# Bias tables of block 1 repeated inside DRAM, all four at the start, and their transfers issued from the GpSimd queue

## Chip, cores and metric

The kernel runs on one core of a Trainium2 chip. The metric is the device time of one execution in microseconds (us). The reference has one batch row of 512 tokens and 1024 features; everything is float32, and products are made exact enough by splitting each operand into a high part (fp32r) and a low part, three matmuls for one.

## The reference, cut to what matters

Block 1 is a layer with three attention branches and a convolutional feed-forward; block 2 has two more layers. The change touches only block 1's attention. Its first branch has three groups of four heads (dilation 1, 4, 16), its second eight heads with a sliding window; to the logits of all of them a bias is added that depends only on the distance between query and key, by a table of 32 buckets:

```python
def band_bias(table, dist):
    return jnp.transpose(table[t5_bucket(dist)], (2, 0, 1)).astype(jnp.float32)

logits = jnp.einsum('nkgbqd,nkbsd->nkgbqs', qb, kw, preferred_element_type=jnp.float32) * SCALE
logits = jnp.where(mask, logits + bias[:, :, None], -jnp.inf)
m = jnp.max(logits, axis=-1)
p = jnp.exp(logits - m[..., None])
```

Queries go in blocks of 128 against the block before and their own, so the bias of one head is a 128 x 256 matrix in which every diagonal is constant.

## The kernel before

The kernel is written with tiles and pools; a scheduler sets the order in which each engine's instructions stand, and each engine then runs its list in order. Weights come in 512 KB pieces (`wraw`, three buffers, line 153) through the queue of SyncE (SP), are split by ScalarE (ACT, line 139, high part) and VectorE (DVE, line 140, low part) and used by TensorE (PE) in `gemm` (line 172). For a branch there are blocks of 256 columns: queries, keys, values. Values are made token-major in `v_direct` (line 576).

The bias comes in three steps. `bias_rows` multiplies a one-hot matrix (`oh`, 198 KB, and `tb`) on PE (line 468) and DVE copies the four results (line 470), one for each kind of head, into a small `row` tile: 4, 4, 4 and 8 heads, 384 distances each. `bias_table` (line 477) writes each row 128 times into a DRAM tile `fd`: with 4 heads 768 KB, with 8 heads 1536 KB. Read with a step one element shorter than a row, it gives a head's matrix (`bias_ap`); `band_bias` (line 817) and the two reads in `attn_a` (lines 752 and 757) bring it into one of two `tmp_bias` buffers. Then DVE adds it to the scaled scores (line 513, or 545 for dilation 4 and 16), takes the maximum (516, 547), ACT exponentiates (485, 550), PE transposes (491) and multiplies with the values (532, 554).

Table 0 is made before group 0, tables 1 and 2 before their groups, table 3 before the third branch, which has no bias itself, and it is read in the second branch. All these transfers are issued from SP, the queue that also issues the weights. `normed` (lines 715 to 721) makes the normalised input again from `num` tiles, which come through SP as well.

Of the kernel before, what the change touches and what calls it, by code (L numbers as in the profile page):

```python
# [65 lines left out]
class Weights:  # L66
    """[128, 512] tiles (high, low) of a [K, c] block, 512 / c rows of 128 in each"""
# [17 lines left out]
class QWeights:  # L85
    """tiles of the quarters (column tile n, rows k < 4 or k >= 4)"""
# [8 lines left out]
class Builder:  # L95
# [41 lines left out]
    def wsplit(self, raw, H, L):  # L137
        """the exact high and low parts"""
        self.nc.scalar.copy(out=H, in_=raw)  # L139
        self.nc.vector.tensor_sub(out=L, in0=raw, in1=H.bitcast(F32))  # L140

    def wtiles(self, raw, pool=None, tag="wq", bufs=4, cols=1024, step=512, back=False):
        """the parts of up to 1024 columns, 512 by 512"""
        pool, m = pool or self.wp, raw.shape[-1]
        t = [pool.tile([P, cols], F32R, name=tag + x, tag=tag + x, bufs=bufs) for x in "HL"]
        for q in sorted(range(0, m, step), reverse=back):
            self.wsplit(raw[:, q:q + step], *[x[:, q:min(q + step, m)] for x in t])
        return [[x[:, q:q + 512] for x in t] for q in range(0, m, 512)]
# [27 lines left out]
    def strassen_y(self, ys, R, keep=False):  # L176
        """the sums of the quarters of y (rows k < 4 and k >= 4, first and second half of the tokens)"""
        nc, h = self.nc, R.n // 2
        a0, b0 = R.off, R.off + h
        A, B = slice(a0, b0), slice(b0, b0 + h)  # L180
        T, todo = {i: [] for i in (1, 2, 3, 4)}, []
        for k in range(4):
            if self.inplace:
                w = self.x[:, k::4]
                q = [w[:, 0, A], lambda w=w: w[:, 1, A], w[:, :, B]]
            else:
                q = [self.first_half(k, A), lambda k=k: self.first_half(k + 4, A), self.half_y[k][:, :, :h]]
            todo.append(self.y_sums(T, k, *q, None if keep else [t[:, B] for t in ys[k]]))
        for rest in todo:
            rest()  # L190
        half = lambda k, s: [ys[k][0][:, s], ys[k][1][:, s]]
        return [[half(k, A) for k in range(4)], [half(k + 4, A) for k in range(4)], [half(k + 4, B) for k in range(4)],
                T[4], T[1], T[2], T[3]]

    def gemm_pairs(self, W, ys, R, use, between=()):
        """all column tiles; the first two advance together, as the last of ys may come late"""
        nk, per, between = len(ys), KD // len(W), list(between)
        for g in ((0, 1), *((t,) for t in range(2, KD))):
            ps = [[(self.psum("o" if t == 4 else "g"), o, m) for o, m in R.segs] for t in g]
            for k in range(nk):  # L200
                yH, yL = ys[k]
                for t, p in zip(g, ps):
                    H, L = W[t // per].at(k, t % per)
                    for i, (a, b) in enumerate(((H, yH), (H, yL), (L, yH))):
                        for q, o, m in p:
                            self.nc.tensor.matmul(q[:, :m], lhsT=a, rhs=b[:, o:o + m],  # L206
                                                  start=(k == 0 and i == 0), stop=(k == nk - 1 and i == 2))
            if between:
                between.pop(0)()
            for t, p in zip(g, ps):  # L210
                use(p, t)
# [9 lines left out]
    def y_sums(self, T, k, a, c, w, q4, pool=None):  # L221
        """a and c: the rows k < 4 and k >= 4 of the first half of the tokens; w: both of the second half"""
# [25 lines left out]
    def strassen(self, src, Y, R, out, last, off=0, mid=None):  # L248
        """[2 * 128 features, tokens] of a block of weights with seven products of quarters (Winograd's form);
        the last product lies among the next block's, and last takes what it gives"""  # L250
# [15 lines left out]
        def product(i, ps=None, tag="g"):  # L266
            """with ps, added to what is there"""
# [42 lines left out]
    def end(self):  # L310
        """the last product of the block before"""
        tail, self.tail = self.tail, None
        if tail:
            tail()
# [12 lines left out]
    def sumsq(self, acc, src, R, k):  # L327
        """acc += src^2"""
# [27 lines left out]
    def bcast(self, rc, R):  # L356
        """rc, a column for each chunk of tokens, as rows in all partitions"""
# [21 lines left out]
    def prenorm(self, gname, defer=True, inplace=False):  # L379
        """y = x * g is split and the reciprocal of the norm is applied to the products (defer), or y is normalised"""  # L380
# [11 lines left out]
    def prenorm_r(self, R):  # L392
        """the reciprocal of the norm, in all partitions"""
# [24 lines left out]
    def halves(self, parts, products, post, nextw, nparts=None):  # L418
        """the last products before a norm, half of the tokens by half; the second half is normalised in the next phase"""
# [36 lines left out]
    # ---------------------------------------------------------------- block 1  # L456
    def bias_rows(self, pool):
        """the bias of each distance, a row for each head"""
        nc, A = self.nc, self.A
        oh = pool.tile([33, 4, 384], F32, name="oh")  # L460
        nc.sync.dma_start(out=oh, in_=A["onehot"])
        tb = pool.tile([33, 20], F32, name="tb")
        nc.vector.memset(tb[32:33], 1.0)
        nc.sync.dma_start(out=tb[:32], in_=A["rel_bias"])
# [8 lines left out]
    def bias_table(self, kind):  # L473
        """each row 128 times, to be read along its diagonals"""
        row, n = self.fd[kind]
        self.fd[kind] = self.dp.tile([n, P, 384], F32, name=f"fd{kind}")
        self.nc.sync.dma_start(out=self.fd[kind], in_=row.unsqueeze(1).to_broadcast([n, P, 384]))

    def bias_ap(self, kind, h, rows, k0, nk):
        a = self.fd[kind][:, :, :]  # L480
        return bass.AP(tensor=a.tensor, offset=a.offset + h * P * 384 + 127 + k0, ap=[[383, rows], [1, nk]])
# [15 lines left out]
    def band_head(self, qT, kT, base, kbase, V, bias, ops, obase, negm, l, sink=None):  # L497
        """q^T, k^T [64 rows, 512] in natural order; V(kb) the [128, 64] block; previous and own block."""
# [36 lines left out]
    def block_head(self, qT, kT, base, V, bias, ops, negm, l):  # L535
        """four independent 128-blocks"""
# [28 lines left out]
    def v_direct(self, W, ys, rcol, d):  # L565
        """values token-major: block b holds tokens b*128.. (d=1) or b::4 (d=4)"""
# [15 lines left out]
    def v_transposed(self, vTs, bufs=3):  # L582
        """[128 features, 512] tiles -> token-major blocks"""
# [9 lines left out]
    def block1(self):  # L593
        nc, tc, A = self.nc, self.tc, self.A
        w0 = []
        with self.phase("qp") as qp, ExitStack() as ctx:
# [20 lines left out]
            with self.phase("at") as at:  # L617
                self.qp, self.qkb = at, 10
                with self.phase("ap") as ap:
                    self.ap = ap  # L620
                    self.bias_rows(ap)
                    self.bias_table(0)
# [43 lines left out]
    def gates(self, Y, gates):  # L666
        """the gates' products, kept in DRAM until the branches are merged"""
# [11 lines left out]
    def post_tile(self, ps, acc, t, R, add):  # L679
        """collects a tile of the sublayer's output, in the place of x, and its squares"""  # L680
# [8 lines left out]
    def postnorm(self, acc, gpost, R, Rn, xold, xnew):  # L689
        """x = xold + norm(x); the next pre-norm of the tokens Rn"""  # L690
# [14 lines left out]
    def attn_a(self, W, ys, rb, rc, oH, oL):  # L705
# [17 lines left out]
        for g, d in enumerate((1, 4, 16)):  # L723
            if g:
                self.bias_table(g)
# [15 lines left out]
            for t in range(2):  # L741
                ops = self.psum("o")
                for u in range(2):
# [5 lines left out]
                    else:  # L749
                        b = self.tmp("bias", 2, 512)  # L750
                        if d == 4:
                            nc.sync.dma_start(out=b[:, :P], in_=self.bias_ap(1, h, P, P, P))
                        else:
                            nc.vector.memset(b[:, :P], NEG)
                            for r in range(4):
                                s = slice(32 * r, 32 * r + 32)
                                nc.sync.dma_start(out=b[s, s], in_=self.bias_ap(2, h, 32, P, 32))
# [26 lines left out]
        nc.sync.dma_start(out=sel, in_=A["sel4"])  # L784
# [29 lines left out]
    def band_bias(self, kind, h):  # L814
        b = self.tmp("bias", 2, 512)
        for u in range(2):
            self.nc.sync.dma_start(out=b[:, 256 * u:256 * u + 256], in_=self.bias_ap(kind, h, P, 0, 256))
        return b

    def attn_b(self, W, ys, oH, oL, pool, gate):  # L820
# [4 lines left out]
        nc.sync.dma_start(out=snk[:, 0], in_=A["sinks"].to_broadcast([P, 8]))  # L825
# [30 lines left out]
    def attn_c(self, W, ys, oH, oL):  # L856
        nc, qp, A = self.nc, self.qp, self.A
        self.bias_table(3)
        tri = self.ap.tile([P, P], F32, name="tri")
        nc.sync.dma_start(out=tri, in_=A["tri"])  # L860
        cm = self.ap.tile([P, P], BF16, name="cm")
        cmf = self.tmp("p", 6, 512)
        nc.sync.dma_start(out=cmf[:, :P], in_=A["cmask"])
# [13 lines left out]
    def stick_pair(self, q, k, V, t, ops, tri, cm):  # L877
        """two heads; the blocks j of 128 keys against the queries from j*128 on lie one after the other"""
# [71 lines left out]
    def conv_ffn(self):  # L950
# [5 lines left out]
        def conv(u, j):  # L956
            """u holds two zeros before the first token"""
# [84 lines left out]
    def last_w(self, src, nk=4, spare=("t3",)):  # L1042
        """nk rows of 128 for all columns, in two blocks; what the ring doesn't hold lies where the sums of y were"""
# [19 lines left out]
    def ffn_order(self, chunks, up, down, last):  # L1063
        """the down products of a chunk lie between the up products of the next one"""
# [15 lines left out]
    def flush(self):  # L1080
        """the elementwise rest of a block follows the products of the next one"""
# [4 lines left out]
    def hidden(self, src, dst):  # L1086
        """the parts of two hidden tiles"""
# [7 lines left out]
    # ---------------------------------------------------------------- block 2  # L1095
# [91 lines left out]
    def first_blocks(self, name, ys, R, gs):  # L1187
        """the first blocks in halves of the tokens, so that the second half has time to be normalised"""
# [135 lines left out]
    def feature_major(self, o, base, R):  # L1324
        """transposes [tokens, 128] blocks; yields (psum, first token, tokens) within the range R"""
# [71 lines left out]
    def stack(self, t, R, key):  # L1397
        """the two maps' exact parts for products of K = 128: the queries' high and low parts against the keys' high
        part twice, and the high part against the keys' low part"""
# [13 lines left out]
    def v_heads(self, ps, rb, c0):  # L1413
        """one head's values, token-major; chunks of 128 tokens, the 16-token chunk is slot 4"""
# [18 lines left out]
    def diff_heads(self, heads, lam, R):  # L1433
        """the steps of the blocks of 128 queries: scores(i + 1), values(i - 1), transposes(i)"""
# [106 lines left out]
class Cols:  # L1541
    """[128, 1] column views: t[:, i] or t[:, i, h]"""
# [11 lines left out]
# ------------------------------------------------------------------ host side: layout and shape-only constants  # L1554
def wblocks(w, c=256):
    """[K, N] -> [N/c, 128, (K/128)*c]"""
# [4 lines left out]
def qblocks(w):  # L1561
    """[1024, N] -> [N/256, 128, (column tile, half of the rows, 4, 128)]"""
# [140 lines left out]
```

## Time and profile before

| | us |
|---|---|
| median of 3 runs | 3174.17 (3173.94 to 3175.4) |
| span of the profiled execution | 3173.5 |
| PE busy | 3105.4 (98%) |
| DVE busy | 2250.6 (71%) |
| ACT busy | 1533.8 (48%) |

The span runs from the first to the last instruction of the profiled execution; the median of the runs lies 0.7 us above it, and the profiled execution's own time is taken as 3174.2. PE is the bound on average, so a change can gain only where PE is idle or runs at the lower clock. In the rows below "x" is a count of instructions, "<-" points from what is written to what is read, and a trailing bracket gives the idle time of the engine before the instruction and what ended it.

### The profile page before, as it was taken

Reading aid. Unit: us, or ns where it says so; the run is one execution under the profiler, and the core shown is the slowest. Engines: PE = TensorE matmul, PEld = TensorE weight load, DVE = VectorE, ACT = ScalarE, POOL = GpSimd, SP = SyncE. Lnnn points to the kernel's source line nnn. Section 1 sums busy time; section 2 is a strip of 40 time slices with the busy share of each in tenths; the row PEclk is TensorE's granted clock in tenths of the full one; section 3 lists DMA queues with packets and bytes.
Section 4 is the critical chain, followed back from the end, with each engine's and each line's share of the span. In section 5 each row is a group of like instructions: output and inputs, shape, how many; then the busy total and the mean of one; then the engine's idle time right before and its main releaser. Section 6 shows DMA issues by size and latency. Waiting matters only on the chain.

```text
span 3173.5 us, 54811 instructions
## 1 busy us (share of the span) xinstructions
PE 3105.4 (98%) x22264; PEld 2872.8 (91%) x22264; DVE 2250.6 (71%) x4225; ACT 1533.8 (48%) x2968; POOL 0.7 (0%) x6
## 2 busy tenths in 40 slices
PE   5899999999999999999999999999999999999998
PEld 4676798988899999999889999999999988899998
DVE  4235777887888797775766777768777576677775
ACT  3345555665455554444553444445444455344443
POOL 0000000000000000000000000000000000000000
PEclk8899999999999999999999999999999999999999
DMA  4421236423233332333212223333233321223332
GB/s 120 95 78 62 81 123 204 145 87 111 89 102 110 102 107 94 107 98 104 66 52 64 87 88 106 94 100 94 94 107 95 107 67 59 67 84 106 96 108 77
DMA packets 102148, 304.36 MB, mean 96 GB/s; under 512 B 12387, under 2 KB 27367, under 8 KB 101896
## 3 DMA queue, kind: packets, MB, share of 16 engines
q1 hardware_dynamic: 98296, 294.38, 30.0%
q10 hardware_dynamic: 3600, 6.49, 0.7%
q8 instruction: 174, 2.85, 0.4%
q14 instruction: 78, 0.64, 0.1%
HBM read 286.41 MB, written 14.42 MB: 95 GB/s over the span
## 4 chain that ended last, share of the span: by engine, by line
PE 93%; DMA 4%; DVE 2%; ACT 1%; issue 0%; SPq 0%; DVEq 0%; ACTq 0%
PE ps_g L172 35%; PE ps_g L278 18%; PE ps_g L276 9%; PE ps_s L172 8%; PE ps_g L206 7%; PE ps_o L276 4%; PE ps_o L206 1%; DMA fd<-row 1%; PE ps_g L576 1%; DMA wraw<-in_w_in 1%; PE ps_s L1467 1%; DMA tmp_bias<-fd 1%; PE ps_s L510 1%; PE ps_s L1524 1%; PE ps_o L1503 1%; PE ps_o L532 1%
## 5 line engine op out<-in xcount | busy, mean ns | idle before, releaser
L140 DVE TENSOR_TENSOR wqL<-wraw,wqH 128x512 fp32r<-128x512 f32 (+1 forms) x676 | 604.8, 910 | 275.3 <-ACT wqH L139 267.4
L139 ACT CAST wqH<-wraw 128x512 fp32r<-128x512 f32 (+1 forms) x676 | 526.7, 796 | 495.6 <-PE ps_g L172 258.6
L172 PE MATMUL ps_g<-yH,wqH 128*128 128x264 f32 (+2 forms) x1520 | 430.4, 322 | 2.3 <-ACT wqH L139 2.2
L172 PE MATMUL ps_g<-yL,wqH 128*128 128x264 f32 (+2 forms) x1520 | 430.8, 321 | 0.4 <-DVE yL L414 0.4
L172 PE MATMUL ps_g<-yH,wqL 128*128 128x264 f32 (+2 forms) x1520 | 430.3, 322 | 0.8 <-DVE wqL L140 0.7
L278 PE MATMUL ps_g<-t,wqH 128*128 128x256 f32 (+1 forms) x1760 | 326.5, 283 | 0.0
L172 PEld LDWEIGHTS ps_g<-yL,wqH 128*128 128x128 f32 x1520 | 264.7, 189 | 24.9 <-issue 5.2
L172 PEld LDWEIGHTS ps_g<-yH,wqL 128*128 128x128 f32 x1520 | 263.1, 189 | 23.4 <-issue 4.1
L172 PEld LDWEIGHTS ps_g<-yH,wqH 128*128 128x128 f32 x1520 | 263.4, 189 | 22.6 <-ACT wqH L139 3.1
L278 PEld LDWEIGHTS ps_g<-t,wqH 128*128 128x128 f32 x1760 | 272.4, 188 | 1.8
L278 PE MATMUL ps_g<-t,wqL 128*128 128x256 f32 (+1 forms) x880 | 248.7, 283 | 0.0
L139 ACT CAST wqH<-ws 128x1024 fp32r<-128x1024 f32 x100 | 105.2, 1052 | 126.8 <-PE ps_o L276 34.3
L278 PEld LDWEIGHTS ps_g<-t,wqL 128*128 128x128 f32 x880 | 166.1, 189 | 0.0
L276 PE MATMUL ps_g<-t,wqH 128*128 128x264 f32 (+1 forms) x800 | 148.5, 283 | 0.0
L172 PE MATMUL ps_s<-hL,wqH 128*128 128x264 f32 (+1 forms) x544 | 141.4, 317 | 0.0
L172 PE MATMUL ps_g<-hL,wqH 128*128 128x264 f32 (+1 forms) x544 | 141.3, 317 | 0.0
L172 PE MATMUL ps_g<-hH,wqL 128*128 128x264 f32 (+1 forms) x544 | 141.2, 317 | 0.0
L172 PE MATMUL ps_s<-hH,wqL 128*128 128x264 f32 (+1 forms) x544 | 141.2, 317 | 0.0
L172 PE MATMUL ps_g<-hH,wqH 128*128 128x264 f32 (+1 forms) x544 | 141.1, 317 | 0.0
L172 PE MATMUL ps_s<-hH,wqH 128*128 128x264 f32 (+1 forms) x544 | 141.0, 317 | 0.0
L258 DVE TENSOR_TENSOR ws<-wraw 128x512 f32<-128x512 f32 x100 | 69.3, 693 | 86.9 <-DMA wraw<-in_ffn_w_gate 34.7
L140 DVE TENSOR_TENSOR wqL<-ws,wqH 128x1024 fp32r<-128x1024 f32 x100 | 122.4, 1224 | 6.6 <-ACT wqH L139 3.1
(434 smaller groups left out, 8207.9 us busy)
## 6 DMA issues: line engine op xcount, KB each, us to landing
wraw<-in_ffn_w_gate SPq DMA_DIRECT2D x88, 512.0 KB, 3.7
wraw<-in_ffn_w_up SPq DMA_DIRECT2D x88, 512.0 KB, 3.7
wraw<-in_ffn_w_down SPq DMA_DIRECT2D x88, 512.0 KB, 3.5
wraw<-in_w_in SPq DMA_DIRECT2D x86, 512.0 KB, 3.8
wraw<-in_w_up SPq DMA_DIRECT2D x64, 512.0 KB, 3.7
wraw<-in_w_down SPq DMA_DIRECT2D x32, 512.0 KB, 3.5
wraw<-in_w_gate SPq DMA_DIRECT2D x24, 512.0 KB, 4.1
tmp_p<-gates ACTq DMA_DIRECT2D x24, 256.0 KB, 3.6
```

The source lines that it names most:

```text
L139: self.nc.scalar.copy(out=H, in_=raw)
L140: self.nc.vector.tensor_sub(out=L, in0=raw, in1=H.bitcast(F32))
L172: self.nc.tensor.matmul(t[:, :m], lhsT=a, rhs=b[:, o:o + m], start=(k == 0 and i == 0), stop=(k == nk - 1 and i == 2))
L206: self.nc.tensor.matmul(q[:, :m], lhsT=a, rhs=b[:, o:o + m], start=(k == 0 and i == 0), stop=(k == nk - 1 and i == 2))
L258: nc.vector.tensor_add(out=S[:, :512], in0=A21, in1=A22)
L276: nc.tensor.matmul(ps, lhsT=a, rhs=b, start=first, stop=last)
L278: nc.tensor.matmul(ps, lhsT=a, rhs=b, start=False, stop=last, skip_group_check=True)
L510: nc.tensor.matmul(ps[:, c], lhsT=q[:, i * P:(i + 1) * P], rhs=k[:, lo * P:(i + 1) * P], start=True, stop=True)
L532: nc.tensor.matmul(ops[obase:obase + 64, i * P:(i + 1) * P], lhsT=V(kb), rhs=pT[:, s0:s0 + P], start=(kb == lo), stop=(kb == i))
L576: nc.tensor.matmul(ps[:, :256], lhsT=a[:, ts], rhs=w, start=(k == 0 and i == 0), stop=(k == KD - 1 and i == 2))
L1467: nc.tensor.matmul(ps[:nq, :e - a], lhsT=qm[r], rhs=k[2][r, a:e], start=False, stop=not dg)
L1503: nc.tensor.matmul(ops[:nq, :P], lhsT=aT[:, j * P:j * P + nq], rhs=V[:, j], start=(j == 0), stop=False)
```

## The change

`bias_table` now makes two transfers. The first brings the row from SBUF into a small DRAM tile `fr` (4 or 8 rows of 384). The second copies from that DRAM tile into `fd`, with a source step of 0 over 128 repeats. `fd` is turned round: 128 repeats outermost, and within each all heads, so that one repeat of a kind with 4 heads is a run of 6 KB. `bias_ap` follows the new layout. All four tables are made at the start, before group 0. These transfers, the reads of the bias and the loads of `oh`, `tb`, `sel`, `tri`, `cmask` and `sinks` are issued from GpSimd (POOL). The diff also takes out docstrings and comments, which make no instruction.

```diff
     def bias_rows(self, pool):
...
-        nc.sync.dma_start(out=oh, in_=A["onehot"])
+        nc.gpsimd.dma_start(out=oh, in_=A["onehot"])
...
-        nc.sync.dma_start(out=tb[:32], in_=A["rel_bias"])
+        nc.gpsimd.dma_start(out=tb[:32], in_=A["rel_bias"])
...
         row, n = self.fd[kind]
-        self.fd[kind] = self.dp.tile([n, P, 384], F32, name=f"fd{kind}")
-        self.nc.sync.dma_start(out=self.fd[kind], in_=row.unsqueeze(1).to_broadcast([n, P, 384]))
+        once = self.dp.tile([n, 384], F32, name=f"fr{kind}")
+        self.nc.gpsimd.dma_start(out=once, in_=row)
+        self.fd[kind] = self.dp.tile([P, n, 384], F32, name=f"fd{kind}")
+        self.nc.gpsimd.dma_start(out=self.fd[kind], in_=once[:, :].unsqueeze(0).to_broadcast([P, n, 384]))
 
     def bias_ap(self, kind, h, rows, k0, nk):
         a = self.fd[kind][:, :, :]
-        return bass.AP(tensor=a.tensor, offset=a.offset + h * P * 384 + 127 + k0, ap=[[383, rows], [1, nk]])
+        n = a.shape[1]
+        return bass.AP(tensor=a.tensor, offset=a.offset + h * 384 + 127 + k0, ap=[[n * 384 - 1, rows], [1, nk]])
...
                     self.bias_rows(ap)
-                    self.bias_table(0)
+                    for kind in range(4):
+                        self.bias_table(kind)
...
         for g, d in enumerate((1, 4, 16)):
-            if g:
-                self.bias_table(g)
...
-                            nc.sync.dma_start(out=b[:, :P], in_=self.bias_ap(1, h, P, P, P))
+                            nc.gpsimd.dma_start(out=b[:, :P], in_=self.bias_ap(1, h, P, P, P))
...
-                                nc.sync.dma_start(out=b[s, s], in_=self.bias_ap(2, h, 32, P, 32))
+                                nc.gpsimd.dma_start(out=b[s, s], in_=self.bias_ap(2, h, 32, P, 32))
...
-            self.nc.sync.dma_start(out=b[:, 256 * u:256 * u + 256], in_=self.bias_ap(kind, h, P, 0, 256))
+            self.nc.gpsimd.dma_start(out=b[:, 256 * u:256 * u + 256], in_=self.bias_ap(kind, h, P, 0, 256))
...
     def attn_c(self, W, ys, oH, oL):
         nc, qp, A = self.nc, self.qp, self.A
-        self.bias_table(3)
...
```

SP's queue in the program's first part, before (fd_223, fd_694 and fd_1051 are tables 0 to 2):

```order
L153 DMA wraw<-in_w_in 128x1024 x2
L477 DMA fd_223<-row 512x1x384
L715 DMA num<-in_x 128x512 x2
L477 DMA fd_694<-row 512x1x384
L817 DMA tmp_bias<-fd_223 128x256 x4
L153 DMA wraw<-in_w_in 128x1024 x2
L817 DMA tmp_bias<-fd_223 128x256 x2
L153 DMA wraw<-in_w_in 128x1024
L817 DMA tmp_bias<-fd_223 128x256 x2
L477 DMA fd_1051<-row 512x1x384
```

And the same place of SP's queue now:

```order
L153 DMA wraw<-in_w_in 128x1024 x2
L719 DMA num<-in_x 128x512 x6
L153 DMA wraw<-in_w_in 128x1024 x3
L719 DMA num<-in_x 128x512 x2
L153 DMA wraw<-in_w_in 128x1024 x21
```

Nothing of the bias is left between the weights and the `num` tiles. POOL's queue, which held no transfer before, now holds these (fr_223 to fr_235 are the rows in DRAM, fd_225 to fd_237 tables 0 to 3):

```order
L477 DMA fr_223<-row 4x384
L477 DMA fr_227<-row 4x384
L477 DMA fr_231<-row 4x384
L477 DMA fr_235<-row 8x384
L479 DMA fd_225<-fr_223 128x1536
L479 DMA fd_229<-fr_227 128x1536
L479 DMA fd_233<-fr_231 128x1536
L479 DMA fd_237<-fr_235 128x3072
L819 DMA tmp_bias<-fd_225 128x256 x8
L754 DMA tmp_bias<-fd_229 128x128 x4
L759 DMA tmp_bias<-fd_233 32x32 x16
```

The first read of the bias stands behind all four tables. DVE's list around the first addition of the bias, before:

```order
L560 TENSOR_TENSOR qk<-ps_g,tmp_rb 128x512
L140 TENSOR_TENSOR wqL<-wraw,wqH 128x1024
L716 SCALAR_TENSOR_TENSOR num<-num,vecs,tmp_rb 128x512 x2
L721 TENSOR_TENSOR yL<-num,yH 128x512 x2
L513 SCALAR_TENSOR_TENSOR tmp_p<-ps_s,tmp_bias 128x384
L513 SCALAR_TENSOR_TENSOR tmp_p<-ps_s,tmp_bias 128x512
```

And the same place of DVE's list now, where line 516 is the addition:

```order
L720 SCALAR_TENSOR_TENSOR num<-num,vecs,tmp_rb 128x512 x2
L563 TENSOR_TENSOR qk<-ps_g,tmp_rb 128x512
L725 TENSOR_TENSOR yL<-num,yH 128x512 x2
L563 TENSOR_TENSOR qk<-ps_g,tmp_rb 128x512
L140 TENSOR_TENSOR wqL<-wraw,wqH 128x1024 x3
L516 SCALAR_TENSOR_TENSOR tmp_p<-ps_s,tmp_bias 128x384
```

The last two `num` tiles moved ahead of the copies of the keys (line 563), and the addition stands behind one more split of a weight.

## Rows read from the trace of the kernel before

**Rows 1.** Busy time of each engine in two stretches, with clock and DMA

```profile
core 0: us, PE busy (x) PEld busy (x) DVE busy (x) ACT busy (x) POOL busy (x), PEclk, DMA share, GB/s
0.00:180.00 180.00, 127.75 (x610) 103.29 (x611) 59.35 (x106) 58.86 (x127) 0.70 (x6) 0.85 0.46 108
...
520.00:3173.00 2653.00, 2640.24 (x19765) 2504.68 (x19763) 1981.12 (x3667) 1294.79 (x2448) 0.00 (x0) 1.00 0.30 95
```

**Rows 2.** Chain that ended last, 0 to 560 us: start, duration, what

```profile
25.55 33.83 DMA fd<-row
59.45 7.13 SPq L817
66.63 24.95 DMA tmp_bias<-fd
...
106.13 26.72 DMA wraw<-in_w_in
```

**Rows 3.** Waits, 0 to 560 us: who for whom, total us, times, longest

```profile
PE ps_s L510 <- DVE tmp_p L513: 41.1, 1, 41.1
...
DVE tmp_p L513 <- DMA tmp_bias<-fd: 28.9, 1, 28.9
...
DVE num L716 <- DMA num<-in_x: 20.1, 1, 20.1
```

**Rows 4.** SP's timeline, 9 to 62 us: start, duration, instruction

```profile
30.88 8.36 SPq L715 DMA_DIRECT2D num<-in_x  x2
39.29 3.75 SPq L477 DMA_DIRECT2D fd<-row  x1
```

**Rows 5.** DMA of 26 to 59 us: GB/s in 40 slices; packets, MB, share

```profile
GB/s 0 44 26 22 26 26 24 24 26 24 24 26 121 166 26 24 47 207 59 26 24 26 26 22 26 26 42 26 26 22 26 26 22 26 26 24 24 34 26 67
...
q1 hardware_dynamic: 756, 1.23, 26.0%
```

**Rows 6.** Busy time in the stretches around PE's waits, columns as in group 1

```profile
51.20:92.30 41.10, 0.00 (x1) 0.00 (x0) 3.36 (x6) 2.52 (x3) 0.00 (x0) 0.53 0.33 60
92.30:106.10 13.80, 13.78 (x47) 9.72 (x48) 8.94 (x21) 7.21 (x25) 0.00 (x0) 0.54 0.42 103
...
131.70:135.20 3.50, 0.77 (x3) 0.30 (x2) 1.22 (x1) 2.09 (x2) 0.00 (x0) 1.00 0.23 93
```

**Rows 7.** Busy time in stretches of 10 us, columns as in group 1

```profile
0.00:10.00 10.00, 1.86 (x4) 1.39 (x5) 3.55 (x13) 5.06 (x9) 0.70 (x6) 1.00 0.81 251
10.00:20.00 10.00, 10.00 (x39) 7.94 (x38) 10.00 (x23) 10.00 (x22) 0.00 (x0) 1.00 1.05 362
...
30.00:40.00 10.00, 10.00 (x53) 8.45 (x52) 9.40 (x14) 3.41 (x6) 0.00 (x0) 1.00 0.30 46
40.00:50.00 10.00, 10.00 (x84) 9.83 (x83) 0.00 (x0) 1.90 (x4) 0.00 (x0) 1.00 0.29 44
```

**Rows 8.** DVE's timeline, 24 to 64 us: the copies of the rows

```profile
24.99 1.22 DVE L470 COPY row<-ps_s 4x384 f32<-4x384 f32 x2
```

**Rows 9.** Issues of 0 to 520 us: count, KB each, median us to landing

```profile
tmp_bias<-fd SPq DMA_DIRECT2D x24, 128.0 KB, 2.5
fd<-row SPq DMA_DIRECT2D x3, 768.0 KB
...
fd<-row SPq DMA_DIRECT2D x1, 1536.0 KB
...
oh<-in_onehot SPq DMA_DIRECT2D x1, 198.0 KB
```

**Rows 10.** Timeline of all engines behind the wait, 62 to 180 us

```profile
91.71 1.16 DVE L513 SCALAR_TENSOR_TENSOR tmp_p<-ps_s,tmp_bias 128x384 f32<-128x384 f32 x2 [28.88 <-DMA tmp_bias<-fd]
...
95.61 0.90 PE L491 MATMUL ps_t<-ident,tmp_p 128*128 128x128 f32 x3
```

**Rows 11.** SP's timeline, 209 to 228 us: the reads for dilation 16

```profile
215.08 3.59 SPq L757 DMA_DIRECT2D tmp_bias<-fd  x8
```

**Rows 12.** DVE's timeline, 209 to 228 us: the addition that they feed

```profile
218.15 0.69 DVE L545 SCALAR_TENSOR_TENSOR tmp_p<-ps_s,tmp_bias 128x512 f32<-128x512 f32 x1 [2.37 <-PE ps_t L491]
```

More of the change, by code (lines that the diff above doesn't have):

```diff
@@ L783, in attn_a @@
         sel = qp.tile([4, 2, P], F32, name="sel")
-        nc.sync.dma_start(out=sel, in_=A["sel4"])
+        nc.gpsimd.dma_start(out=sel, in_=A["sel4"])
         for t in range(2):
@@ L824, in attn_b @@
         snk = qp.tile([P, 2, 8], F32, name="snk")
-        nc.sync.dma_start(out=snk[:, 0], in_=A["sinks"].to_broadcast([P, 8]))
+        nc.gpsimd.dma_start(out=snk[:, 0], in_=A["sinks"].to_broadcast([P, 8]))
         nc.vector.tensor_scalar(out=snk[:, 1], in0=snk[:, 0], scalar1=-1.0, scalar2=None, op0=ALU.mult)
@@ L857, in attn_c @@
         nc, qp, A = self.nc, self.qp, self.A
-        self.bias_table(3)
         tri = self.ap.tile([P, P], F32, name="tri")
-        nc.sync.dma_start(out=tri, in_=A["tri"])
+        nc.gpsimd.dma_start(out=tri, in_=A["tri"])
         cm = self.ap.tile([P, P], BF16, name="cm")
         cmf = self.tmp("p", 6, 512)
-        nc.sync.dma_start(out=cmf[:, :P], in_=A["cmask"])
+        nc.gpsimd.dma_start(out=cmf[:, :P], in_=A["cmask"])
         nc.vector.tensor_copy(out=cm, in_=cmf[:, :P])
```

## Prediction

> **What bounds it now.** I first read the busy times by stretch [rows 1]. In the first 180 us PE is busy for 127.75, so 52.3 us of its idle time lie there; in the 2653 us from 520 on it is idle for 12.8. The change touches only the first part, and only there is there much to win. The chain that ended last says what the idle time waits for [rows 2]: at 25.55 a transfer that fills table 0 (33.83 us), then SP's issue of the reads (7.13), then the read of the bias (24.95). The waits show the same from PE's side [rows 3]: one wait of 41.1 us at line 510 for DVE's addition at line 513, and behind that DVE's wait for the bias. SP's own list shows why it lasts so long [rows 4]: table 1 is issued at 39.29, ahead of the reads of table 0, and an issue that normally takes under a microsecond takes 3.75. From 26 to 59 us hardly anything but tables moves, at 24 to 26 GB/s, and the 16 DMA engines are busy for 26.0% of the time, which is four of them [rows 5]. Elsewhere the same engines moved 362 GB/s [rows 7]. So the bias is late because a table trickles, twice: once as itself, and once as table 1, ahead of the reads.
>
> PE is then idle from 51.2 to 92.3, and the stretch of 13.8 us behind it runs at a granted clock of 0.54, the lower level of 1.2 GHz for nearly all of it [rows 6]. A second hole follows at 131.7 to 135.2, where PE is busy for 0.77 of 3.50 us; the chain puts it on a weight of 512 KB that took 26.72 us to come, in the queue behind table 2 [rows 2, 6].
>
> **The change, part by part.** All times are on the profiled execution's span, 3173.5; its 0.7 us up to the median is added at the end.
>
> The wait for the first bias goes: -41.1 [rows 3]. What stands in its place is computed below.
>
> The late weight: SP's queue holds no table any more, so the weight has only its own way to go: -2.7, the idle part of 3.50 us [rows 6]. The 20.1 us for which DVE waited for `num` [rows 3] lie inside the 41.1 and give nothing more.
>
> The early load of `oh`: 198 KB [rows 9] now travel among the first weights and inputs, in a stretch that moved 251 GB/s [rows 7]; before, they came behind them. PE starts on those inputs, so this delays it by 198 KB / 251 GB/s = 0.8 us at most; I take 0.7, with 0 as the lower bound.
>
> The new way of the bias, step by step. The first row is copied at 24.99 + half of 1.22 = 25.6 [rows 8]. The write of the row to DRAM is then issued; POOL issues no transfer before, so the cost of an issue there is unknown. SP's issues bound it: 0.45 (a read at dilation 16, 3.59 for eight [rows 11]) and 3.75 [rows 4]; I take 1 us, nearer to the undisturbed one. The landing takes 2.5, like that of a 128 KB bias read [rows 9]. So table 0 can be issued at 29.1, and its data move from 30.1. Behind it POOL issues tables 1 to 3 before the first read of the bias, and each transfer's parts queue on the same DMA engines, so I let that read wait for all four tables: 3 x 768 + 1536 = 3840 KB or 3.93 MB [rows 9]. Their rate is the unknown that decides. The trace has no copy inside DRAM. The upper bound is 362 GB/s [rows 7]: 10.9 us. The lower bound is the rate of the only transfer that reads one small source again and again, 25 GB/s [rows 5]: 157 us. I take 181, half the upper one, since each byte is both read from DRAM and written to it: 21.7 us. It is nearer to the upper bound because the new copy has 128 repeats to spread over the engines and does not read from a few SBUF partitions. At that rate the engines are half free, and `num` and the weights of SP pass beside the tables. The tables end at 51.8, the read of the bias lands 2.5 later at 54.3, and from the addition (91.71) to the first transposes (95.61) it is 3.9 [rows 10]: PE goes on at 58.2. It is ready for it at 51.2 + 0.7 = 51.9. So a wait of 6.3 us remains: +6.3, bounds 0 and 142 (30.1 + 157 + 2.5 + 3.9 = 193.8).
>
> The trace shows that a hole of 41.1 us has a mean clock of 0.53 [rows 6], so the clock falls some 2.5 us after PE stops; a hole of 6.3 us will bring the lower level too. I therefore book nothing for the 13.8 us at 0.54. Without a hole they would shrink: PE's part by up to half, 6.9; as DVE and ACT alternate with PE there, I take 4.5 for that case.
>
> The rule "Use all 16 engines" (the Trainium skill, DMA: Bandwidth & Descriptors, Rules for kernel authors) says that the outermost dimension sets how many engines a transfer gets, at most 4 with four copies outermost and all 16 with 128. The trace agrees with the first half, 26.0% of 16 engines [rows 5]. If each engine kept its pace and only their number grew, the rate would be 100 GB/s; that is a rival below. The same page (Latency and other measured facts) states 207 GB/s for copies inside DRAM; no run here shows it, and by it the tables would take 19.0 us and the sum would come to an estimated 3137.
>
> Issue by POOL of the later reads: at dilation 16 a head needs four small reads. SP issued eight in 3.59 us [rows 11], and DVE's addition at 218.15 then waited for PE and not for them [rows 12]. At 1 us each, the four reads of the third head end 2 us later and reach that addition; +2, bounds 0 and 5 for two heads. The reads of the other kinds are issued two heads ahead and lie under the products; without that cover each pair would cost 2 us. `sel`, `tri`, `cmask` and `sinks` come early or under other work: 0. The order of the instructions behind block 1's attention changes in small ways; PE is 99.5% busy there [rows 1], and I book 0.
>
> Sum: 3173.5 - 41.1 - 2.7 + 0.7 + 6.3 + 2.0 = 3138.7, and with 0.7 up to the median 3139.4, so 3139, 1.1% below 3174.17.
>
> **The rivals.**
>
> *The bias comes in time.* At 362 GB/s the way is 30.1 + 10.9 + 2.5 + 3.9 = 47.4, before 51.9. Then no hole is left and the clock stays up: 3173.5 - 41.1 - 2.7 - 4.5 + 0.7 + 2 + 0.7 = 3128.6. For it speaks that 362 was reached in this very program; against it that DRAM carries each byte twice.
>
> *The tables stay slow, or start late.* At 100 GB/s (four times the 25 of four engines) they take 39.3 us, PE goes on at 75.8, the wait is 23.9 and the time 3139.4 + 17.6 = 3157. For it speaks that the pace of one engine, 25 / 4 = 6 GB/s, is far below 362 / 16 = 23, and the rows don't say whether the source or the engine makes it so. A late start gives much the same: DVE is busy for 9.40 of the 10 us from 30 to 40 and for 0 from 40 to 50 [rows 7]; if POOL could not issue while DVE works, the tables would start at 41 and PE would go on at 41 + 21.7 + 6.4 = 69.1, a wait of 17.2, 3150. The Trainium skill has a rule for this (SBUF — State Buffer, Who interferes with whom): descriptors of transfers issued from GpSimd can't be written while DVE holds the port pair that the two share; it also says that operations with two SBUF inputs, which DVE mostly runs there, take only the read side.
>
> *The tables are slower than before in sum.* All 16 engines read the same 6 KB. If that source can give no more than the one of before, 25 GB/s, the first read waits for 157 us of tables, where before it waited for two: a wait of 142 us, 3139.4 + 135.7 = 3275. It decides from the point where the new wait eats the whole gain: 41.1 + 2.7 - 0.7 - 2 = 41.1 us of wait, so tables of 56.5 us, 70 GB/s. For it speaks that making all tables first puts 3.93 MB ahead of the first read instead of 1.57; against it that the source is now DRAM.
>
> *The weights gain nothing.* The hole at 131.7 could come from the split of the weights and not from the queue: 3139.4 + 2.7 = 3142.
>
> **How the numbers follow.** I give 0.50 to the forecast (its own range 3131 to 3147), 0.22 to the bias in time, 0.15 to slow or late tables, 0.10 to tables slower than the point of decision and 0.03 to the weights. The range of 3123 to 3160 leaves out the slow end of the third case and all of the fourth, and the fast tail, about 0.18 together. Some 0.2%, 6 us, is what a measurement of this kernel can tell from no change: faster needs less than 3168, which holds for the first three, the last and nearly all the slow-table cases, 0.87; 0.03 lies around the point of decision, 0.10 above.
>
> **What would show it.** Right: PE's wait at line 513 (510 before) falls from 41.1 to under 15 us; no transfer of 33 us stands in the chain; from 30 to 52 us the DMA rate is well over 150 GB/s; PE's hole at 131.7 is gone. Wrong: tables in flight beyond 60 us; a wait of POOL's reads at dilation 16 in DVE's list; a clock that is down although PE has no hole; or a new wait of DVE for the `num` tiles near 38 us, which now stand ahead of the copies of the keys.

## The result and the profile after

| | before | after |
|---|---|---|
| median of 4 runs, us | 3174.36 | 3139.25 (3133.03 to 3141.62) |
| ratio, 95% interval | | 0.9885 (0.9873 to 0.9897) |
| span of the profiled execution | 3173.5 | 3131.2 |
| PE busy | 3105.4 (98%) | 3101.2 (99%) |

The forecast of 3139 is met. Two later sets of four runs gave 3139.9 and 3136.8. The runs of the changed kernel spread over 8.6 us here; those of the kernel before stay within 1.5 in this set and within 2.8 to 5.2 in the three later ones. The profiled execution is the run of 3133.03, the quickest of the four.

Busy time by stretch of the changed kernel, columns as in [rows 1]:

```profile
30.00:40.00 10.00, 8.17 (x37) 6.47 (x35) 6.44 (x11) 4.25 (x7) 4.27 (x8) 1.00 0.81 257
40.00:50.00 10.00, 7.65 (x30) 6.51 (x31) 7.12 (x10) 0.62 (x1) 0.00 (x0) 0.66 0.87 296
50.00:60.00 10.00, 10.00 (x83) 9.50 (x82) 4.22 (x8) 7.72 (x17) 1.06 (x2) 1.00 0.49 184
...
100.00:140.00 40.00, 39.69 (x203) 35.21 (x203) 8.71 (x13) 14.76 (x46) 5.04 (x10) 1.00 0.16 51
0.00:180.00 180.00, 167.13 (x834) 134.69 (x834) 72.93 (x123) 81.64 (x184) 22.42 (x48) 0.98 0.39 130
```

In the first 180 us PE is idle for 12.9 us, where it was 52.3 [rows 1]. The 41.1 us [rows 6] are gone, and so is the hole at 131.7: from 100 to 140 only 0.31 us are left. But there is a new hole near 40 (from 38.2 to 42.4), and behind it PE runs at the lower level of its clock from 43.0 to 49.9 (0.66 in the mean of that slice). The waits of 30 to 62 us name it (columns as in [rows 3]):

```profile
DVE num L720 <- DMA num<-in_x: 4.5, 2, 2.5
...
PE ps_g L579 <- DVE qk L563: 4.2, 1, 4.2
DVE tmp_p L516 <- DMA tmp_bias<-fd: 1.9, 1, 1.9
```

DVE's 28.9 us for the bias [rows 3] are 1.9 now, and PE does not wait for the bias at all. It waits 4.2 us for DVE's copies of the keys (L563), which stand in DVE's list behind the last two `num` steps (L720), whose tiles have not come. The chain that ended last passes through the same tile (start, duration, what):

```profile
31.33 9.59 DMA num<-in_x
40.94 0.75 DVE num L720
41.69 0.61 DVE qk L563
```

Why the tile needs 9.6 us is seen in the DMA view of 30 to 48 us. The first row is GpSimd's queue: packets, MB, share of all 16 engines; the others are issues, with the median time to landing:

```profile
q0 software_dynamic: 703, 4.31, 70.6%
...
fd<-fr POOLq DMA_DIRECT2D x3, 768.0 KB, 9.6
fd<-fr POOLq DMA_DIRECT2D x1, 1536.0 KB, 16.8
...
num<-in_x SPq DMA_DIRECT2D x2, 256.0 KB, 8.3
tmp_bias<-fd POOLq DMA_DIRECT2D x4, 128.0 KB, 11.5
```

All four tables are issued before the two tiles have landed, and the packets of the first three (31.5 to 42.6 us) share the engines with the tiles. POOL's timeline (start, duration, instruction, idle time before it) has the issues:

```profile
30.23 2.11 POOL L479 DMA_DIRECT2D fd<-fr  x4 [1.33 <-DMA fr<-row]
37.42 2.17 POOL L819 DMA_DIRECT2D tmp_bias<-fd  x4 [5.08 <-DMA fd<-fr]
```

An issue of a table costs 0.53 us on POOL. The table packets lie between 31.5 and 48.3 us: 3.93 MB in 16.8 us, 234 GB/s.

### The profile page after: what moved, and what is told of

It reads as the page before. It is cut to its first block, busy times and chain, and to the rows that moved or that the text cites. A ratio compares the mean times of both kernels' runs of the same rounds, so it can differ in the third digit from the quotient of the medians.

```text
span 3131.2 us, 54851 instructions
## 1 busy us (share of the span) xinstructions
PE 3101.2 (99%) x22264; PEld 2869.7 (92%) x22264; DVE 2250.4 (72%) x4225; ACT 1534.7 (49%) x2968; POOL 30.9 (1%) x64
## 4 chain that ended last, share of the span: by engine, by line
PE 95%; DMA 2%; DVE 1%; ACT 1%; issue 0%; ACTq 0%; SPq 0%; DVEq 0%
PE ps_g L172 35%; PE ps_g L278 18%; PE ps_g L276 9%; PE ps_s L172 8%; PE ps_g L206 7%; PE ps_o L276 5%; PE ps_g L579 2%; PE ps_o L206 1%; DMA tmp_p<-gates 1%; PE ps_s L1468 1%; PE ps_s L513 1%; PE ps_o L535 1%; PE ps_s L1525 1%; PE ps_o L1504 1%; PE ps_o L1534 1%; PE ps_t L494 1%
```

## The experiments

There are twelve runs in three sets, each set with the kernel before in it (medians 3175.2 to 3175.7). My theory at the start was that the table's transfer was slow and is fast now, and that this is the gain. The first rival was that the gain comes from taking transfers out of SyncE's queue.

### Which part of the change carries the gain

**e5_pool_only** takes the kernel before and changes the queue alone.

```diff
-        self.nc.sync.dma_start(out=self.fd[kind], in_=row.unsqueeze(1).to_broadcast([n, P, 384]))
+        self.nc.gpsimd.dma_start(out=self.fd[kind], in_=row.unsqueeze(1).to_broadcast([n, P, 384]))
```

and so for the reads and constants. 

> The kernel before with one part of the change alone: its tables as they were (row read from SBUF 128 times by four engines) and where they were, but these transfers, the reads and the constants issued from the GpSimd queue. Theory that the rate of the table's transfer is what was slow: table 0 still takes about 34 us and table 1 stands ahead of the reads, now in the GpSimd queue, so that TensorE still waits some 40 us for the first bias; only the late weight at 131.7 goes. The second four reads stand behind table 2 now and could wait too: 3165 to 3185. Rival, that the shared queue was what was slow (the reads were stuck behind other issues): the reads land right behind table 0 at about 62 and TensorE goes on near 66, 25 to 30 us earlier: 3140 to 3150.

Measured: 3202.4 us, ratio 1.0090 (1.0072 to 1.0108). The queue alone makes the kernel slower by 0.9%, outside both expectations. Waits of 20 to 100 us:

```profile
POOL tmp_bias L817 <- DMA fd<-row: 57.6, 1, 57.6
...
DVE num L716 <- DMA num<-in_x: 45.6, 2, 34.2
...
PE ps_g L576 <- DVE qk L560: 45.3, 1, 45.3
```

The first read waits 57.6 us for its table, as the theory said. What it did not say is that the `num` tiles, now issued beside two slow tables, come after 45 us and stop PE earlier, at 38, in the same place as the hole of the changed kernel. The order changed too: the scheduler put the first addition of the bias at 179.6 us, behind the next products, so that PE's wait for the bias itself is not seen in this run. GpSimd's queue, 30 to 80 us:

```profile
q0 software_dynamic: 544, 1.35, 48.1%
```

That is eight engines' worth of time instead of four [rows 5], for much the same rate: 1.35 MB in 50 us, 27 GB/s, in packets of 4608 bytes that took 1300 ns each (24 to 26 GB/s before). Two tables are in flight in this stretch. From 100 to 110 us it is table 2 alone:

```profile
q0 software_dynamic: 50, 0.23, 22.6%
```

So each table of four rows has four engines' worth, and two tables side by side moved little more (27 GB/s) than one alone (23). The source is the limit; whether that is the repeated reading or the few SBUF partitions that hold the rows was not tried.

**e7_four_outer** keeps DRAM as the source and undoes the layout.

```diff
-        self.fd[kind] = self.dp.tile([P, n, 384], F32, name=f"fd{kind}")
+        self.fd[kind] = self.dp.tile([n, P, 384], F32, name=f"fd{kind}")
...
```

> The changed kernel with the table's layout undone: one row still goes to DRAM and is copied inside DRAM, but with the 4 (8) heads outermost and the 128 repeats within, runs of 1536 bytes. This parts the source (DRAM instead of SBUF partitions) from the spread over the engines. If the source is what was slow, the rate stays as in the changed kernel, over 200 GB/s, and so does the time within 3 us. If the number of engines counts, four engines at the pace seen in the changed kernel (6144 bytes in 234 ns, 26 GB/s each at best) give at most 100 GB/s: 3.93 MB take 40 us or more, the first read lands at 72 or later, TensorE waits 20 us or more: 3155 to 3190. If the pace of one engine too is that of before (1536 bytes in 225 ns, 27 GB/s for four), the tables take 145 us and the time is 3240 to 3270. I expect the middle one.

Measured: 3137.1 us, beside 3136.8 of the changed kernel in the same set; the 3155 to 3190 that I expected did not come. Its issues, 32 to 54 us:

```profile
q0 software_dynamic: 2955, 4.34, 69.2%
...
fd<-fr POOLq DMA_DIRECT2D x1, 1536.0 KB, 21.4
```

The equal time says little about the layout, because the scheduler changed the order too. DVE's timeline of 139 to 141 us:

```profile
139.75 1.15 DVE L515 SCALAR_TENSOR_TENSOR tmp_p<-ps_s,tmp_bias 128x384 f32<-128x384 f32 x2
```

That is the first addition of the bias, 90 us later than in the changed kernel, so a late bias could not be seen here. The hole near 40 is 2.5 us long, and a second one of 2.6 us comes at 137.7, with 13.6 us at half clock behind it. What the run shows is the pace: 4608 bytes from a DRAM row took 181 ns in the median, 25 GB/s for one engine, where the same packet from SBUF took 1300 ns in e5 with two tables in flight and some 720 with one. The 69% are four tables in flight at once; up to 34.5 us, with the first alone, some four packets run at a time. So the source sets the pace of an engine. What the layout is worth in the end time is not shown, least of all from SyncE's queue: there the transfers kept to four engines although table 1 had been issued at 39.29 [rows 4, 5].

**e6_sp_issue** undoes the queue alone: every `gpsimd.dma_start` of the changed kernel is `sync.dma_start` again.

> The changed kernel with one part undone: all the transfers that it issues from GpSimd are issued from SyncE again, tables still copied inside DRAM over 128 repeats and all at the start. Theory that the transfer's rate is what counts: tables take about 17 us as in the changed kernel, most of the gain stays; what SyncE loses is the issue of the next weights and of the last two num tiles, which stand behind the tables and reads: 3133 to 3152. Rival, that the queue is what counts: weights and num tiles are held up for the time of the tables and the reads, 3152 to 3175.

Measured: 3128.4 us (3123.3 to 3132.8), ratio 0.9851 (0.9835 to 0.9868), and again, in **e12_sp_issue_again**, 3130.3.

> The kernel of e6_sp_issue again, in the same job as the others: 3123 to 3133 as before, 0 to 4 us below e9_num_pool by its earlier start (0.7 to 0.8 us) and the cheaper reads of the bias.

In the set of e6 the changed kernel took 3136.8, so the queue part of the change costs some 8 us, and the rival has fallen: the gain does not come from the queue. These 8 us hold a change of order too. In e6 the scheduler put both copies of the keys ahead of the last two `num` steps, which then wait without stopping PE. DVE's timeline of 30 to 64 us:

```profile
46.20 1.50 DVE L720 SCALAR_TENSOR_TENSOR num<-num,vecs,tmp_rb 128x512 f32<-128x512 f32 x2 [7.01 <-DMA num<-in_x]
```

### What the spread of the runs is, and the new hole

**e1_after_again** and **e8_after_third** are the changed kernel itself.

> The changed kernel once more, to see what its runs differ in: four runs of it lay between 3133.0 and 3141.6 us, where the kernel before stayed within 1.5. My theory: the spread is made in the first 60 us, where the copies of the tables, the weights and the num tiles share the 16 DMA engines, so the num tiles land at 37.7 and 40.9 in one run and some us later in another, and the hole on TensorE (4.17 us in the first profile, with 6.8 us at half clock behind it) is longer. Then a second profile with a longer time has a longer hole before 60 us and the same distances from there on. Rival: the spread lies in the merge of the branches or later (waits for the gates); then the landmark at 60 us is the same and the difference comes after 500. Expected median 3133 to 3142.

> The changed kernel as the base of this job: 3133 to 3142, with a hole on TensorE of 4 us or more near 38 us and none at 131.

Medians 3139.9 and 3136.8, spans of the profiles 3138.2 and 3137.4. The waits of 30 to 62 us in e8:

```profile
DVE num L720 <- DMA num<-in_x: 11.7, 2, 6.2
...
PE ps_g L579 <- DVE qk L563: 10.0, 1, 10.0
```

The same program has a hole of 4.2, 10.8 and 10.0 us in three profiles. The 1000th matmul starts at 218.7, 227.4 and 228.0, so most of the spread is made here. The second profile shows a merge that is faster by 2.3 us and the third by 3.2 than the first, so a little lies there too, the other way.

**e2_num8** gives the `num` tiles eight buffers instead of six, so all loads are issued before the tables.

```diff
-                x = self.ap.tile([P, SEQ], F32, name="num", tag="num", bufs=6)
+                x = self.ap.tile([P, SEQ], F32, name="num", tag="num", bufs=8)
```

> Two more buffers for the num tiles, so that all eight loads of x are issued before the tables start to move; the order of VectorE's list stays as it is. Theory: the new hole of 4.17 us at 38.2 and the 6.8 us at half clock behind it (some 3.4 us lost) come from the last two num tiles, which land in 9.6 us beside the tables. Then the hole goes and the transposes could start 7.6 us earlier, at 51.2; the first bias addition at 49.4 then becomes the last to come and holds them to about 53.5, so 4 to 7 us less than the changed kernel in the same job. Rival: the num tiles are late whatever is done since VectorE itself is behind; then a gain under 1.5 us.

Measured: 3138.6 us, no gain, but not for the rival's reason. PE's hole at 38 is gone. Now the bias is last: DVE waits 3.6 us for it, and PE has holes of 0.5 us at 54.1 and 1.7 us at 55.9. Then the clock:

```profile
50.00:60.00 10.00, 7.76 (x54) 6.46 (x53) 5.09 (x9) 8.75 (x20) 0.94 (x2) 0.96 0.52 197
60.00:70.00 10.00, 10.00 (x32) 5.96 (x30) 3.22 (x8) 2.81 (x11) 1.07 (x2) 0.50 0.30 103
70.00:80.00 10.00, 10.00 (x41) 6.73 (x40) 3.75 (x9) 5.24 (x16) 1.07 (x2) 0.69 0.05 13
```

From 59.1 to 76.2 PE works at the lower level. The holes are small, but they lie ahead of the softmax stage, where PE, DVE and ACT take turns, and there the clock stays down for 17 us.

**e3_keys_first** writes the key products ahead of `normed` in the code.

```diff
-            if g == 0:
-                normed(range(8))
             k = [self.qk_evac(self.gemm(wk, n, ys, R1), rb, d) for n in range(2)]
+            if g == 0:
+                normed(range(8))
```

> The key products and their copies are written ahead of the num tiles, so that the first key copy stands ahead of the last num additions in VectorE's list (the second key copy stays behind them). Theory that the hole is a matter of VectorE's order: the first key copy no longer waits, and TensorE's hole at 38.2 falls from 4.17 us to under 2; time 2 to 6 us below the changed kernel of the same job. Rival: the second key copy still waits for the last num tile, so that the hole only moves; same time within 1.5 us.

Measured: 3138.0, 1.9 below the changed kernel of the set and within its spread. PE still waits 9.7 us at L579, for the second key copy. The rival holds.

**e9_num_pool** moves both key copies ahead, by loading the last two tiles later, from GpSimd's queue behind the tables.

```diff
-                nc.sync.dma_start(out=x, in_=A["x"][:, j])
+                (nc.gpsimd if j > 5 else nc.sync).dma_start(out=x, in_=A["x"][:, j])
```

> The changed kernel, but the last two num tiles are loaded from the GpSimd queue behind all the tables, that is later than now; the scheduler then puts VectorE's two key copies ahead of the last two num additions. All else, the GpSimd queue included, is as in the changed kernel. Theory: TensorE's hole of 4 to 11 us near 38 is only a matter of VectorE's order, since the num additions that wait for tiles caught among the tables hold up the key copies and with them TensorE's banks; then the hole goes although the tiles come later, and the time comes to 3124 to 3133, as with the SyncE queue (3128.4). Rival: the GpSimd queue itself costs the time (a slower start of its transfers); then the time stays at 3134 to 3142, or rises since the tiles come later.

Measured: 3139.7. My theory that DVE's order alone makes the loss falls; the time is where the rival had it. Waits of 20 to 100 us:

```profile
ACT wqH L139 <- DMA wraw<-in_w_in: 8.1, 1, 8.1
...
PE ps_s L513 <- DVE tmp_p L516: 7.1, 1, 7.1
```

Now a weight is caught among the tables; its split stands ahead of the bias addition in DVE's list, and PE waits 7.1 us there, at 51.4. Behind it:

```profile
60.00:70.00 10.00, 10.00 (x27) 5.85 (x27) 4.67 (x10) 3.25 (x13) 2.10 (x4) 0.50 0.39 126
70.00:80.00 10.00, 10.00 (x32) 6.53 (x32) 3.03 (x8) 3.53 (x12) 0.53 (x1) 0.50 0.03 7
```

**e10_num_pool_oh** also loads `oh` and `tb` from SyncE.

```diff
-        nc.gpsimd.dma_start(out=oh, in_=A["onehot"])
+        nc.sync.dma_start(out=oh, in_=A["onehot"])
...
```

> As e9_num_pool, and the one-hot matrix and the small table are loaded from SyncE again, behind the inputs, where they were before the change. Theory: the early 198 KB of the GpSimd queue delay TensorE's start; the start was at 8.36 to 8.73 us in the profiles with the early load and at 7.69 and 8.14 without, so 0.3 to 0.8 us less than e9. Rival: the rows of the bias come later by it and so do the tables; then 0 to 2 us more than e9.

Measured: 3140.4, no better than e9. In its profile PE starts at 7.72 instead of 8.68, and there is a hole of 3.8 us at 52.9, again for the bias addition, and the clock is at the lower level from 54.7 to 75.2.

### Fewer tables first

**e4_old_places** keeps copy and queue and makes each table where it was made before.

```diff
-                    for kind in range(4):
-                        self.bias_table(kind)
+                    self.bias_table(0)
...
         for g, d in enumerate((1, 4, 16)):
+            if g:
+                self.bias_table(g)
...
```

> Tables made with the new copy and from the GpSimd queue, but each where it was made before: two tables instead of four stand ahead of the first read of the bias. My prediction made the first read wait for all four tables. Theory from the trace of after: the bias is in time with four tables (no wait of TensorE for it), so that fewer tables ahead gain nothing there; the first bias addition comes some 8 us earlier, and the num tiles are hindered less (hole 2 to 4 us instead of 4.17): 0 to 4 us less than the changed kernel in the same job. Rival: making all tables first is what the gain rests on; then at least 5 us more than the changed kernel.

Measured: 3129.7 us, ratio 0.9858 (0.9843 to 0.9873), 10.2 below the changed kernel of the same set; my 0 to 4 was too little. **e11_sp_old** is the same from SyncE's queue, and so differs from the kernel before in the new copy alone: the row through DRAM, with the layout that goes with it.

> Only the new copy inside DRAM, with all transfers from SyncE and each table where it was made before the change: the least edit that holds what the runs so far say the gain rests on. Theory: the gain is the table's source alone, so this is as good as the tables first from SyncE: 3122 to 3133. Rival: with the tables between the weights in SyncE's list, weights of the later groups are late (as at 131.7 in the kernel before); then 3133 to 3142.

Measured: 3124.4 us (3123.2 to 3126.1), ratio 0.9839 (0.9824 to 0.9854), the best version and below the changed kernel's interval. So the new copy alone holds the whole gain; its source and its layout were not tried apart here. Two stretches of e11:

```profile
40.00:50.00 10.00, 9.35 (x77) 8.99 (x76) 6.59 (x11) 4.44 (x13) 0.00 (x0) 1.00 0.81 263
50.00:60.00 10.00, 10.00 (x67) 7.50 (x65) 6.41 (x12) 6.72 (x18) 0.00 (x0) 1.00 0.97 315
```

Compare the two profiles of one program with all tables first, e6 and then e12, in the same place:

```profile
50.00:60.00 10.00, 9.05 (x42) 5.44 (x41) 8.07 (x20) 8.38 (x21) 0.00 (x0) 1.00 0.41 127
60.00:70.00 10.00, 10.00 (x61) 7.50 (x62) 4.64 (x9) 7.71 (x24) 0.00 (x0) 1.00 0.34 117
```

```profile
50.00:60.00 10.00, 8.51 (x22) 5.14 (x21) 5.88 (x13) 6.16 (x11) 0.00 (x0) 0.62 0.44 142
60.00:70.00 10.00, 10.00 (x29) 6.26 (x27) 4.11 (x8) 5.28 (x20) 0.00 (x0) 0.50 0.19 63
```

PE is idle for 0.95 us in e6 and for 1.49 in e12, and this half microsecond goes along with 20 us at half clock and a span longer by 11 us (3121.5 and 3132.5). The mean granted clock of each of the eight runs of this program agrees: 0.997 in the four of 3123.3 to 3126.8 us, 0.994 or 0.995 in the four of 3131.6 to 3134.3.

The accounts of the profiles: PE's first start, its idle gaps over 0.4 us up to the 1000th matmul, the time that it works at half clock in the first 130 us (the clock record less the gaps), and the start of that matmul. The order of the products is not the same in all of them.

| profile | start | gaps | half clock | 1000th |
|---|---|---|---|---|
| before | 8.14 | 41.1 + 2.2 + 0.5 + 0.7 | 12.8 | 263.7 |
| after | 8.36 | 4.2 | 6.8 | 218.7 |
| e1, again | 8.50 | 10.8 | 7.8 | 227.4 |
| e8, again | 8.73 | 10.0 | 11.6 | 228.0 |
| e2, eight buffers | 8.62 | 0.5 + 1.7 | 20.5 | 224.2 |
| e3, keys first | 8.39 | 9.7 + 0.6 | 5.8 | 224.6 |
| e7, four outermost | 8.53 | 2.5 + 2.6 | 10.2 | 226.5 |
| e9, tiles behind tables | 8.68 | 7.1 | 26.1 | 229.5 |
| e10, and `oh` from SyncE | 7.72 | 3.8 | 21.9 | 225.7 |
| e4, two tables first | 8.55 | 0 | 6.8 | 215.4 |
| e6, SyncE | 7.69 | 0.9 | 0 | 211.9 |
| e12, SyncE again | 7.96 | 1.5 | 20.1 | 221.8 |
| e11, SyncE, two tables | 8.15 | 0.7 | 0 | 212.6 |

From e6, each line follows by its later start, its larger gaps and half of its time at half clock, within 2.6 us: for e8, 211.9 + 1.0 + 9.1 + 5.8 = 227.8. The exception is e7, 4.5 us above this sum; its 13.6 us at half clock behind the second gap lie beyond the 130 us.

## Why the prediction was right, and where it was not

The number was right; the path to it was right in its first half and wrong in the second. That the total came out so close is luck: a wait booked in one place did not come, and one of nearly the same size came in another that was booked at nothing. With the terms measured below, the first profile comes to -41.1 - 2.7 + 0.2 + 4.2 - 3.0 = -42.4 (its span is 42.3 shorter) and e1 to -41.1 - 2.7 + 0.4 + 10.8 - 2.5 = -35.1 (35.3 shorter).

*The wait for the first bias goes (-41.1) and so does the late weight (-2.7).* Both as said. e11, which has the new copy and nothing else of the change, shows both gone, with no gap over 0.7 us.

*The early load of `oh` (+0.7).* Nine profiles with the early load start at 8.36 to 8.73, 8.55 in the mean; five without at 7.69 to 8.15, 7.93 in the mean: 0.6.

*The tables' rate (181 GB/s) and the remaining wait for the bias (+6.3).* The tables moved at 234 GB/s, between the two bounds, an issue took 0.53 us and not 1, and the first addition came at 49.4 instead of 54.3. The order was as predicted: the first read was issued at 37.42, but its packets moved from 45.9 on, behind nearly all of the tables. The Trainium skill (DMA: Bandwidth & Descriptors, Latency and other measured facts) gives 207 GB/s for copies between DRAM tensors with rows of 16 KiB, 512 KiB apart, from the SyncE or ScalarE queue; the measurement, of another shape and beside other traffic, is above it, and it decides. So the rival that the bias comes in time was right on its mechanism, at two thirds of its rate.

*"At that rate the engines are half free, and num and the weights of SP pass beside the tables."* This is the step that failed. The engines were busy for 0.81 to 0.87 of the stretch, 70.6% by GpSimd's queue alone, and what stood ahead of the key copies in DVE's list came late: a hole of 4.2 to 10.8 us where I had booked 6.3 for the bias. My list of signs held this wait, but I gave it no price and no chance. e2 and e9 show that it is not the `num` tile as such: with that out of the way the bias or a weight is late. In e4 and e11, with two tables instead of four ahead, no gap over 0.7 us is left.

*The clock (0).* The 12.8 us of work at half clock before are gone, worth 6.4, and 6.8 to 11.6 us of it stand in the profiles of the changed kernel, costing 3.4 to 5.8. The net is -0.6 to -3.0, small here. As a rule it was wrong: in e2, e9 and e12 the clock is the largest loss, 10 to 13 us behind holes of 1.5 to 7.1. Nor is the 2.5 us from PE's stop to the fall of the clock, taken from one hole, the same elsewhere: it was 4.8 us in the first profile of the changed kernel (stop at 38.2, fall at 43.0) and 2.4 in e9.

*The reads at dilation 16 (+2).* The wait that I listed is there, and costs nothing. DVE's timeline of 150 to 190 us:

```profile
174.12 0.69 DVE L548 SCALAR_TENSOR_TENSOR tmp_p<-ps_s,tmp_bias 128x512 f32<-128x512 f32 x1 [2.96 <-DMA tmp_bias<-fd]
```

PE shows no gap over 0.3 us there.

*The other rivals.* Slow tables for want of engines: that rival kept each engine at 25 / 4 = 6 GB/s, but the pace rose with the DRAM source, to 6144 bytes in 234 ns, 26 GB/s. The rule "Use all 16 engines" of the Trainium skill (DMA: Bandwidth & Descriptors, Rules for kernel authors), at most four engines with four rows outermost, agrees with [rows 5] and with e5: 22.6% of the engines for one table and 48.1% for two. A late start because of DVE: POOL issued all four tables in 2.11 us at 30.23, in a stretch where DVE was busy for 6.4 of 10 us. Tables slower in sum did not come with the DRAM source (234 GB/s); in e5, with the old source, the kernel is slower.

What stays open is why GpSimd's queue costs 5 to 8 us against SyncE's with the same tables (e4 and e11, e8 and e6). A start later by 0.6 is measured, but e10, which takes that back on top of e9's edit, gains nothing against e9; the tables are issued at 30.2 instead of 27.9, their last packet ends at 48.3 instead of 43.8 (e6), and they move beside the weights instead of in one line with them. These were not tried apart, nor was the order of DVE's list that came with SyncE's queue.

## What to carry to other kernels

When a change removes a wait by moving much data at once, price the next tile that this traffic catches, whichever it is; here three candidates in turn (an input tile, the bias, a weight) took the place of the one removed. Move in a busy stretch only what is read next: two tables instead of four were worth 4 to 10 us. And take a bundle apart: here the new copy held the whole gain, and the queue and the early tables cost time. When a part is undone, look whether the order of the instructions stayed: in e5 and e7 it did not, and e7 could not say what the layout is worth.

## What the runs showed of the hardware that I had not expected

- Reading a few SBUF rows again and again gave 23 to 27 GB/s, whether four engines' worth were busy with it, in 1536-byte packets of 225 ns, or eight, in 4608-byte packets of 1300 ns. The same 4608 bytes from a DRAM row took 181 ns.
- Two tables of four rows each, issued from GpSimd's queue, ran side by side on four engines' worth each (e5, 48.1%). From SyncE's queue the share stayed at 26.0% with both issued [rows 5].
- Issuing a table took 0.53 us on POOL with the 128 repeats outermost and 1.1 us with the four rows outermost (4.40 us for four in e7).
- In five of the profiles (e2, e4, e7, e8, e10) the clock fell to the lower level at about 28 us and stayed there for 3.4 to 6.8 us without any gap over 0.4 us on PE, which was at the end of the eight products of L468. In the others, which run the same products, it did not fall.
- Two profiles of one program (e6 and e12) differ by half a microsecond of idle time on PE ahead of the softmax stage, and by 20 us at half clock behind it. That the one causes the other is read from the order of the two, not tried.
